# Expert results added through 0/1 lists in two fp32r passes, whole-tile places for weights, and the check for longer lists moved between two pairs

## The chip, the core and the metric

The kernel runs on one core of one Trainium2 chip. The metric is the device time of one execution in microseconds (us); smaller is better. Three runs of the kernel before gave a median of 688.06 us (687.87 to 689.03).

## What is computed

The reference is one layer of an encoder on 256 tokens of width 1024: a token mixer (two attention-like branches, merged and normalised), then a mixture of 16 experts. Only the second half is touched here:

```
logits = x @ router_w + router_b; probs = softmax(logits)
g_sel  = group of 4 experts that holds the largest prob
top 2 experts inside that group; their two gates are renormalised to sum 1
expert e on its rows xr:  h = silu(xr @ w1[e]) * (xr @ w3[e]);  y = h @ w2[e]
y_moe[token] = sum over its two experts of gate * y
x = layer_norm(ALPHA * x + y_moe)
```

All arrays are float32. Each expert has three 1024 x 1024 matrices, 12.6 MB, so that the sixteen experts are 201 MB of weights that are read once.

## The kernel before

**Front.** The first 240 us compute the mixer. There the matmuls run on fp32r operands: a number is split into a high part (rounded to fp32r) and a low remainder, and three matmuls (high by high, high by low, low by high: lines 186 to 188 and 199 to 201) replace one fp32 matmul.

**Experts.** The experts are done in eight pairs (loop over `e` = 0, 2, ..., 14, from about line 1454). Each expert has room for S = 64 tokens. `find(e)` (line 1252, VectorE) writes for the pair a tile `oneh` of 128 tokens x 256: for each of two token tiles and each of the pair's two experts, a 1 where the token's place in the expert's list equals the column. `gather` (line 1260) multiplies the tokens by these 0/1 columns, so that the pair's 128 rows lie as columns in `xg`. `gate_lists` (line 1275, VectorE) then multiplies the 0/1 lists by the gates, and `turn_lists` (lines 1280 and 1281) transposes them into `GT`. `up(e, m)` (line 1288) multiplies the rows of one expert by w1 (m = 0) or w3 (m = 2): 16 matmuls of 64 rows x 512 columns, whose two halves lie in the two column halves of the array. ScalarE and VectorE make the gated product `sg`, `turn_pe` (line 1296) transposes it, and ScalarE copies it to `hT`. `down(e, half)` (line 1305) multiplies by w2 into two PSUM banks `py`. These are copied to `y[0]` by ScalarE (line 1492) and `y[1]` by VectorE (line 1493), and in the next pair, after its first `up`, `combine` (line 1313) adds GT times y to the four accumulators `acc`: four fp32 matmuls of 128 x 512.

In the trace every fp32 matmul is two instructions (32 for one `up`, 8 for `combine`); an fp32r matmul is one.

**Weights.** A pair needs twelve tiles of 128 x 4096 (2 MB each): four for each expert's `up`, then four for `down`. There are eleven places for such tiles: three in `ring`, and one each in EA, E0, E1, E2, E3, GA, P1 and X. Five of them (E0, E1, E3, P1, X) are pools of four tiles of 128 x 1024. `load_exp(place)` (lines 846 to 875) takes the next tile of a fixed order into a place that has just been read for the last time: one transfer of 2 MB (rows of 16 KB; line 874), or, in a place of four tiles, four transfers of 512 KB (rows of 4 KB; `load_parts`, line 901). All are issued on the queue of SyncE (SP), in this order. The tile before the last four comes in four transfers (line 872), and the last four (w2 of experts 14 and 15) come in 24 smaller ones in turns (line 863), the last sixteen of 256 KB.

**Tail.** The last pair's `down2(c, fs)` (line 1324) makes the result in three column blocks, c = 0, 1, 2; `combine2(c)` (line 1331) adds each, and the final normalisation follows block by block (lines 1500 to 1550).

**Longer lists.** An expert can have more than 64 tokens. `gates` computes a flag `cfl` for that early. After `down2(0)` (line 1495) four engines load the flag into a register, and `tc.If` (line 1498) jumps over `more_slots()`, which handles the longer lists, when there are none. With the reference's data there are none. Seven places are named as its work space. A hint for the jump stands some instructions ahead of it (`mark_branch_hint_location`, line 1478).

The two lines of the loader that matter most:

```
elif pl in parts4:
    load_parts(e, m, pl, 4)
```

Of the kernel before, what the change touches and what calls it, by code (L numbers as in the profile page):

```python
# [25 lines left out]
LAST = NE - 2  # L26
# [19 lines left out]

@with_exitstack
def trunk(ctx: ExitStack, tc: tile.TileContext, x, cst_d, rows_d, wf, we, lvl_d, out):
# [16 lines left out]
    E0 = ctx.enter_context(tc.tile_pool(name="e0", bufs=4))  # L65
# [782 lines left out]
    def load_exp(pl, n=1):  # L848
        for _ in range(n):
# [15 lines left out]
            elif pl in parts4:  # L865
                load_parts(e, m, pl, 4)
            else:
                t = pl.tile([128, 4096], F32, name="w", tag="w")
                exl[e, m] = [t[:, i * 1024:(i + 1) * 1024] for i in range(4)]
                if nxt[0] == len(order) - 5:  # L870
                    for i in range(4):
                        nc.sync.dma_start(exl[e, m][i], we[e, m, :, i * 1024:(i + 1) * 1024])
                else:
                    nc.sync.dma_start(t, we[e, m])
# [6 lines left out]

    def slot(pl):

        if pl in parts4:
            return [part(pl) for _ in range(4)]
        t = pl.tile([128, 4096], F32, name="w", tag="w")
        return [t[:, i * 1024:(i + 1) * 1024] for i in range(4)]

    def part(pl):
        return pl.tile([128, 1024], F32, name="w", tag="p4" if pl is P1 else "w", bufs=4)  # L890
# [86 lines left out]
    def phase3():  # L977
# [3 lines left out]
        late["E1"] = ctx.enter_context(tc.tile_pool(name="e1", bufs=4))  # L981
# [27 lines left out]
    def phase4():  # L1009
# [3 lines left out]
        late["E3"] = ctx.enter_context(tc.tile_pool(name="e3", bufs=4))  # L1013
        load_exp(late["E2"])
        fr[14] = [late["E3"].tile([128, 1024], F32, name="w", tag="w") for _ in range(4)]
# [156 lines left out]
    hiT = [HI.tile([128, 512], F32, name=f"e{i}", tag="hi") for i in range(4)]  # L1172
    xg = [t.rearrange("p (k s) -> p k s", s=128) for t in hiT[0:2]]
    oneh = hiT[2][:, 0:256].rearrange("p (t a s) -> p t a s", t=2, a=2)
    oneh2 = hiT[2][:, 0:256].rearrange("p (t s) -> p t s", t=2)
    GT = hiT[2][:, 256:512].rearrange("p (t s) -> p t s", t=2)
    sg, hT, y = hiT[3], loT[0:2], loT[2:4]
    acc = [[bank("s" if tt else "o", [128, 512], f"acc{tt}{nh}") for nh in range(2)] for tt in range(2)]

    def residual(tt):  # L1180

        for nh in range(2):
            t = y[nh].rearrange("p (k s) -> p k s", s=128)
# [8 lines left out]
    def residual_add(tt):  # L1192
        for nh in range(2):
            t = y[nh].rearrange("p (k s) -> p k s", s=128)
# [104 lines left out]
    def down(e, half, py):  # L1299
        for f in range(4 * half, 4 * half + 4):  # L1300
            c0 = (f % 4) * 128 + (f // 4) * 64
            for nh in range(2):
                for a in range(2):
                    wt = exl[e + a, 4 + f // 4][f % 4]
                    PE.matmul(py[nh][64 * a:64 * a + 64, :], hT[a][:, c0:c0 + 64], wt[:, nh * 512:nh * 512 + 512],  # L1305
                              start=f == 0, stop=f == 7)
        for a in range(2):
            load_exp(home[e + a, 4 + half])

    def combine(start):  # L1310
        for tt in range(2):
            for nh in range(2):
                PE.matmul(acc[tt][nh], GT[:, tt, :], y[nh], start=start, stop=False, skip_group_check=True)  # L1313


    def down2(c, fs):
# [8 lines left out]
        if fs[-1] == 7:  # L1325
            A.copy(y[1][:, c * 256 - 256:c * 256] if c else y[0], W["y"])  # L1326

    def combine2(c):
        cs = slice(c * 256 - 256, c * 256) if c else slice(0, 512)
        for tt in range(2):  # L1330
            PE.matmul(acc[tt][c > 0][:, cs], GT[:, tt, :], y[c > 0][:, cs], start=False, stop=True,  # L1331
# [4 lines left out]
    def norm_params():  # L1336
# [3 lines left out]
        homes = [ring] * 3 + [EA, late["E2"], late["GA"]]  # L1340
        homes += parts4
        for p in (pl, home[LAST, 5], home[LAST + 1, 5]):
            homes.remove(p)
        par["w"] = homes
# [11 lines left out]
    def more_slots():  # L1356
# [4 lines left out]
        sh = sm[:, 64:66]  # L1361
        for e in range(NE):
            for m in range(6):
                for i in range(4):
                    G.dma_start(wt[m][i], we[e, m, :, i * 1024:(i + 1) * 1024])
            for b in range(2):
# [18 lines left out]
                V.tensor_copy(t2[:, 2:4, :], pg)  # L1385
                for fh in range(2):
                    h = {}
                    for m in (0, 2):
                        h[m] = bank("g", [128, 512])
                        for k in range(8):  # L1390
                            c = fh * 512
                            PE.matmul(h[m], t1[:, k, :], wt[m + k // 4][k % 4][:, c:c + 512], start=k == 0, stop=k == 7)
                    A.activation(sgm, h[0], AF.Sigmoid)
                    V.tensor_mul(hh, h[0], sgm)
                    V.tensor_mul(hh, hh, h[2])
# [3 lines left out]
                    V.tensor_copy(t3[:, 4 * fh:4 * fh + 4, :], pt)  # L1399
                for nh in range(2):  # L1400
                    py = bank("g", [128, 512])

                    n = 2 if e >= LAST and nh else 1
                    for q in range(n):
                        for f in range(8):
                            w = wt[4 + f // 4][f % 4][:, nh * 512:nh * 512 + 512]
                            if e >= LAST:
                                w = wt[5][2 * q + f // 4][:, f % 4 * 256:] if nh else wt[4][f // 2][:, f % 2 * 512:]
                            PE.matmul(py[:, q * 256:(q + 1) * 512 // n], t3[:, f, :], w[:, 0:512 // n],
                                      start=f == 0, stop=f == 7)  # L1410
                    V.tensor_copy(yb, py)
# [215 lines left out]
```

## Time and profile before

| what | value |
|---|---|
| median of 3 runs | 688.06 us (687.87 to 689.03) |
| profiled execution, its own time | 689.79 us |
| its span, first to last instruction | 688.0 us |
| mean granted TensorE clock | 0.991 of 2.4 GHz |
| TensorE matmul busy | 657.4 us (96%) |
| VectorE, ScalarE, GpSimd busy | 205.6, 187.7, 75.9 us |
| bytes moved by DMA | 238.71 MB, mean 347 GB/s |

A busy TensorE is not a TensorE at its peak: matmuls are pipelined and their ends are modelled. "Idle before, releaser" names what ended the idle time ahead of an instruction. The DMA share is the busy share of the core's sixteen DMA engines. SPq rows are issues of transfers, not the transfers themselves.

### The profile page before, as it was taken

The numbers are of one execution on the slowest core, as the hardware profiler recorded it, in microseconds if no ns is written. First come the engines' busy times: TensorE is split into PE (matmuls) and PEld (weight loads), VectorE is DVE, ScalarE is ACT, GpSimd is POOL, SyncE is SP. The second block draws the span as 40 slices with busy tenths as digits, with TensorE's granted clock in tenths as the row PEclk, the third lists the DMA queues.
The fourth block names the chain that finished last, engine by engine and source line by source line (L and its number), as shares of the span: only waits on it lengthen the run. The fifth ranks groups of instructions, "written<-read, shape, count | busy, mean of one in ns | idle before, by whom it ended". The sixth has DMA issues, their size and how long they took to land. (4 is left out here: it accounts for less than half of the span.)

```text
span 688.0 us, 9379 instructions
## 1 busy us (share of the span) xinstructions
PE 657.4 (96%) x3715; PEld 380.5 (55%) x3715; DVE 205.6 (30%) x469; ACT 187.7 (27%) x389; POOL 75.9 (11%) x74
## 2 busy tenths in 40 slices
PE   7999999999999999999999999999999998899976
PEld 6897988999989634344434433433533532334323
DVE  6788846454585311001001001001000100100015
ACT  5764466777464210120121100100100100011111
POOL 1113364431271000000000000000000000000001
PEclk9999999999999999999999999999999999999989
DMA  8969335538879699999999999999999999999971
GB/s 327 399 259 354 127 116 181 197 123 316 317 271 403 214 370 419 397 421 422 413 419 419 419 413 421 427 407 426 422 409 423 426 409 424 419 417 416 404 248 62
DMA packets 40517, 238.71 MB, mean 347 GB/s; under 512 B 4496, under 2 KB 4624, under 8 KB 32400
## 3 DMA queue, kind: packets, MB, share of 16 engines
q1 hardware_dynamic: 40464, 238.02, 86.5%
q8 instruction: 32, 0.52, 0.3%
q14 instruction: 21, 0.17, 0.1%
HBM read 236.95 MB, written 1.05 MB: 346 GB/s over the span
## 5 line engine op out<-in xcount | busy, mean ns | idle before, releaser
L1288 PE MATMUL g<-w,e 128*64 128x512 f32 x992 | 222.3, 598 | 3.5 <-DMA w<-in_we_dram 3.5
L1288 PEld LDWEIGHTS g<-w,e 128*64 128x64 f32 x992 | 69.7, 137 | 140.7 <-issue 126.9
L1305 PE MATMUL g<-w,f 128*64 128x512 f32 x448 | 105.7, 595 | 0.0
L166 DVE TENSOR_TENSOR lo<-w,hi 128x512 fp32r<-128x512 f32 x87 | 67.7, 789 | 51.0 <-ACT hi L165 50.1
L165 ACT CAST hi<-w 128x512 fp32r<-128x512 f32 x117 | 70.2, 618 | 39.2 <-PE g L200 31.8
L199 PE MATMUL g<-xp,hi 128*128 128x256 f32 x256 | 74.3, 290 | 0.0
L201 PE MATMUL g<-xp,lo 128*128 128x256 f32 x256 | 72.5, 283 | 0.2 <-DVE lo L166 0.2
L200 PE MATMUL g<-xp,hi 128*128 128x256 f32 x256 | 72.4, 283 | 0.0
L1305 PEld LDWEIGHTS g<-w,f 128*64 128x64 f32 x448 | 38.9, 137 | 56.5 <-issue 50.2
L166 POOL TENSOR_TENSOR lo<-w,hi 128x512 fp32r<-128x512 f32 x33 | 45.2, 1371 | 110.7 <-ACT hi L165 110.7
L1537 POOL TENSOR_TENSOR e<-e,par 128x256 f32<-128x256 f32 x2 | 1.4, 727 | 462.3 <-DVE nmr L1533 462.3
L199 PEld LDWEIGHTS g<-xp,hi 128*128 128x128 f32 x256 | 48.9, 191 | 2.6 <-issue 1.4
L201 PEld LDWEIGHTS g<-xp,lo 128*128 128x128 f32 x256 | 49.0, 191 | 0.4 <-DVE lo L166 0.4
L200 PEld LDWEIGHTS g<-xp,hi 128*128 128x128 f32 x256 | 49.0, 191 | 0.0
L1493 DVE COPY f<-g 128x512 f32<-128x512 f32 x7 | 4.8, 691 | 112.0 <-PE g L1305 112.0
L1260 PEld LDWEIGHTS g<-e,raw 128*128 128x128 f32 x224 | 26.1, 191 | 20.0 <-DVE e L1252 10.2
L1260 PE MATMUL g<-e,raw 128*128 128x128 f32 x224 | 28.7, 281 | 8.1 <-DVE e L1252 8.1
L1271 ACT ACTIVATE e<-g,cst 128x128 f32<-128x128 f32 x28 | 10.5, 456 | 64.5 <-PE g L1260 64.5
L1475 DVE TENSOR_TENSOR e<-e,g 128x512 f32<-128x512 f32 x8 | 5.5, 687 | 73.5 <-ACT e L1474 73.5
L1485 ACT COPY f<-g 128x512 f32<-128x512 f32 x8 | 4.7, 585 | 82.6 <-PE g L1296 82.6
L1313 PE MATMUL acc<-f,e 128*128 128x512 f32 x56 | 25.9, 605 | 0.0
L1462 DVE TENSOR_TENSOR e<-e,g 128x512 f32<-128x512 f32 x8 | 5.5, 688 | 64.1 <-PE g L1288 64.1
(316 smaller groups left out, 736.2 us busy)
## 6 DMA issues: line engine op xcount, KB each, us to landing
w<-in_we_dram SPq DMA_DIRECT2D x49, 2048.0 KB, 17.5
w<-in_we_dram SPq DMA_DIRECT2D x178, 512.0 KB, 11.0
w<-in_wf_dram SPq DMA_DIRECT2D x13, 2048.0 KB, 8.7
w<-in_wf_dram SPq DMA_DIRECT2D x8, 512.0 KB, 10.1
w<-in_we_dram SPq DMA_DIRECT2D x16, 256.0 KB, 5.6
rbc<-in_rows_dram SPq DMA_DIRECT2D x1, 1036.0 KB, 15.6
f<-in_we_dram SPq DMA_DIRECT2D x4, 256.0 KB, 7.1
out_dram<-par SPq DMA_DIRECT2D x4, 256.0 KB, 2.1
```

The costliest lines, as they stand in the source:

```text
L165: A.copy(hi, src)
L166: (G if on_pool(u) else V).tensor_sub(lo, src, hi.bitcast(F32))
L199: PE.matmul(p, hi[:, w], rh(k), start=k == 0, stop=False)
L200: PE.matmul(p, hi[:, w], rl(k), start=False, stop=False)
L201: PE.matmul(p, lo[:, w], rh(k), start=False, stop=k == nk - 1)
L1260: PE.matmul(p[:, i, :], raw[:, tt, k * 128:(k + 1) * 128], oneh2[:, tt, :], start=tt == 0, stop=tt == 1)
L1271: A.activation(t[:, i, :], p[:, i, :], AF.Identity, bias=C("b1")[:, 4 + i:5 + i], scale=C("g1")[:, 4 + i:5 + i])
L1288: PE.matmul(h[64 * nh:64 * nh + 64, :], xg[kh][:, k, 64 * (e % 2):64 * (e % 2) + 64], wcol(e, m + kh, k, nh), start=kh + k == 0, stop=kh = ...
L1305: PE.matmul(py[nh][64 * a:64 * a + 64, :], hT[a][:, c0:c0 + 64], wt[:, nh * 512:nh * 512 + 512], start=f == 0, stop=f == 7)
L1313: PE.matmul(acc[tt][nh], GT[:, tt, :], y[nh], start=start, stop=False, skip_group_check=True)
L1462: V.tensor_mul(sg, sg, h)
L1475: V.tensor_mul(sg, sg, h)
```

## The change

- E0, E1 and E3 become a `Place` each: one tile of 128 x 4096 with four parts. From the eighteenth tile of the order on (`WHOLE`), they are loaded by one transfer of 2 MB; P1 and X stay in four parts. By the order of the loader 21 tiles change from four transfers to one.
- The lists stay 0/1 and are held as fp32r (exactly). The gates are no longer multiplied into them (`gate_lists` is gone). Instead `turn_lists` multiplies the lists by the gate columns on TensorE (two matmuls with 2 columns), and ScalarE copies the gates of the 128 rows into `gs` (two copies of 64 x 1).
- `put_y(nh)` takes a half of the result out of PSUM, times `gs`, as a high part (ScalarE) and a low part (VectorE), both fp32r. `combine(nh)` adds it with four fp32r matmuls. The first half is added between the two halves of the next pair's `up(e, 0)`, the second after them.
- `find(e + 2)` moves ahead of `up(e + 1, 2)`.
- The check for longer lists moves from the tail to between pair 10 and pair 12 (`CHECK` = 12), behind both `combine`s, without the hint. Its work space is the two places of the w2 tiles (10, 5) and (11, 5), one in `ring` and P1; they are loaded again only after it. `more_slots` is rewritten to do with two places.

```
+class Place:
+    def __init__(self, ctx, tc, name):
+        self.t = ctx.enter_context(tc.tile_pool(name=name, bufs=1)).tile([128, 4096], F32, name="w")
+        self.at = 0
+    def part(self):
+        i, self.at = self.at, (self.at + 1) % 4
+        return self.t[:, i * 1024:(i + 1) * 1024]
...
-            elif pl in parts4:
+            elif pl in parts4 and (pl in (P1, X) or nxt[0] < WHOLE):
                 load_parts(e, m, pl, 4)
+            elif pl in parts4 and nxt[0] != len(order) - 5:
+                exl[e, m] = pl.parts()
+                nc.sync.dma_start(pl.t, we[e, m])
...
-    def gate_lists(e):
-        V.tensor_tensor(oneh, oneh, gw[:, :, e:e + 2][:, :, :, None].to_broadcast([128, 2, 2, S]), op=OP.mult)
-
-    def turn_lists():
-        p = bank("g", [128, 2, 128])
+    def turn_lists(e):
+        p = bank("g", [128, 260])
         for tt in range(2):
-            PE.transpose(p[:, tt, :], oneh2[:, tt, :], ident)
-        A.copy(GT, p)
+            PE.transpose(p[:, tt * 128:(tt + 1) * 128], oneh2[:, tt, :], ident)
+        for tt in range(2):
+            PE.matmul(p[:, 256:258], oneh2[:, tt, :], gw[:, tt, e:e + 2], start=tt == 0, stop=tt == 1)
+        A.copy(GT, p[:, 0:256].rearrange("p (t s) -> p t s", t=2))
+        for a in range(2):
+            r = slice(64 * a, 64 * a + 64)
+            A.copy(gs[r], p[r, 256 + a:257 + a])
...
+        if (e, half) == (CHECK - 2, 1):
+            return
         for a in range(2):
             load_exp(home[e + a, 4 + half])
-    def combine(start):
+    def put_y(nh):
+        if nh == 0:
+            y["h"], y["l"] = two("y", F32R)
+        A.activation(y["h"], py[nh], AF.Identity, scale=gs)
+        V.scalar_tensor_tensor(y["l"], py[nh], gs, y["h"].bitcast(F32), op0=OP.mult, op1=OP.subtract)
+
+    def combine(nh, start):
         for tt in range(2):
-            for nh in range(2):
-                PE.matmul(acc[tt][nh], GT[:, tt, :], y[nh], start=start, stop=False, skip_group_check=True)
+            for i in "hl":
+                PE.matmul(acc[tt][nh], GT[:, tt, :], y[i], start=start and i == "h", stop=False, skip_group_check=True)
...
+    def check_slots():
+        over = nc.values_load(cfl, engines=(ET.PE, ET.Activation, ET.DVE, ET.Pool), min_val=0, max_val=1)
+        pls = [home[CHECK - 2 + a, 5] for a in range(2)]
+        sl = [slot(pl) for pl in pls]
+        with tc.If(over > 0):
+            more_slots(*sl)
+        for pl in pls:
+            load_exp(pl)
...
     for e in range(0, NE, 2):
-        h = up(e, 0) if e else h0
+        if e == CHECK:
+            combine(0, False)
+            put_y(1)
+            combine(1, False)
+            check_slots()
+            h = up(e, 0)
+        elif e:
+            h = up(e, 0, (0,))
+            combine(0, e == 2)
+            put_y(1)
+            up(e, 0, (1,), h)
+        else:
+            h = h0
         A.activation(sg, h, AF.Sigmoid)
         V.tensor_mul(sg, sg, h)
-        if e:
-            combine(e == 2)
-        gate_lists(e)
+        if e not in (0, CHECK):
+            combine(1, e == 2)
...
+        if e < LAST:
+            find(e + 2)
         h = up(e + 1, 2)
-        if e == LAST:
-            tc.mark_branch_hint_location("slots", "LikelyTaken", engines=ENG4)
         V.tensor_mul(sg, sg, h)
         if e < LAST:
-            find(e + 2)
             p = gather(0)
...
-            A.copy(y[0], py[0])
-            V.tensor_copy(y[1], py[1])
+            put_y(0)
+    y[0], y[1] = two("y")
     down2(0, range(8))
-    over = nc.values_load(cfl, engines=(ET.PE, ET.Activation, ET.DVE, ET.Pool), min_val=0, max_val=1)
-    wt = [slot(pl) for pl in par["w"][0:7]]
-    tm = wt.pop()
-    with tc.If(over > 0, label="slots"):
-        more_slots()
     A.activation(sm[:, 90:91], eps_in[:, 0:1], AF.Sqrt)
```

## Rows read from the trace of the kernel before

**Rows 1.** The page, its parts 1 and 2: busy time, DMA share in 40 slices.

```profile
PE 657.4 (96%) x3715; PEld 380.5 (55%) x3715; DVE 205.6 (30%) x469; ACT 187.7 (27%) x389; POOL 75.9 (11%) x74
...
DMA  8969335538879699999999999999999999999971
```

**Rows 2.** Windows: stretch, length, busy by engine, PEclk, DMA share, GB/s.

```profile
250.00:653.00 403.00, 390.60 (x1852) 159.68 (x1850) 39.83 (x65) 43.35 (x93) 0.00 (x0) 1.00 1.01 417
...
560.00:575.00 15.00, 15.00 (x62) 5.16 (x61) 1.71 (x3) 0.97 (x2) 0.00 (x0) 1.00 1.02 408
575.00:590.00 15.00, 11.55 (x50) 3.67 (x50) 0.69 (x1) 1.18 (x2) 0.00 (x0) 0.90 1.02 428
653.00:668.00 15.00, 10.86 (x42) 4.13 (x39) 0.00 (x0) 2.07 (x3) 0.00 (x0) 0.81 0.86 300
```

**Rows 3.** Timeline of SP, 540 to 575 us: start, length, issues of weight transfers.

```profile
540.76 30.33 SPq L901 DMA_DIRECT2D w<-in_we_dram  x16
572.04 2.89 SPq L874 DMA_DIRECT2D w<-in_we_dram  x3
```

**Rows 4.** Timeline, 480 to 600 us: TensorE's pair 10 and its waits.

```profile
500.25 7.04 PE L1288 MATMUL g<-w,e 128*64 128x512 f32 x32
...
534.05 2.05 PE L1260 MATMUL g<-e,raw 128*128 128x128 f32 x16 [1.13 <-DVE e L1252]
...
553.18 7.04 PE L1288 MATMUL g<-w,e 128*64 128x512 f32 x32
...
585.88 5.35 PE L1288 MATMUL g<-w,e 128*64 128x512 f32 x16 [3.45 <-DMA w<-in_we_dram]
```

**Rows 5.** Timeline of TensorE's weight loads around one combine, 506 to 511 us.

```profile
506.26 0.14 PEld L1288 LDWEIGHTS g<-w,e 128*64 128x64 f32 x2 [0.28 <-issue]
507.22 0.30 PEld L1313 LDWEIGHTS acc<-f,e 128*128 128x128 f32 x2 [0.81 <-issue]
...
510.85 0.20 PEld L1288 LDWEIGHTS g<-w,e 128*64 128x64 f32 x4 [0.76 <-DMA w<-in_we_dram]
```

**Rows 6.** Timeline of TensorE in the front: fp32r matmuls, 512 columns.

```profile
105.09 0.39 PE L188 MATMUL g<-hi,xp 128*128 128x512 f32 x1
105.31 0.39 PE L186 MATMUL g<-hi,xp 128*128 128x512 f32 x1
```

**Rows 7.** Groups by line and shape: busy us, mean ns, idle before.

```profile
L1066 PE MATMUL g<-wg,rT 128*128 128x16 f32 x32 | 3.7, 258 | 0.0
...
L1456 ACT ACTIVATE e<-g 128x512 f32<-128x512 f32 x8 | 4.8, 597 | 49.6 <-PE g L1288 49.6
...
L1548 DVE SCALAR_TENSOR_TENSOR par<-par,sm,g 128x512 f32<-128x512 f32 x2 | 1.5, 732 | 0.0
```

**Rows 8.** Timeline of the tail, 657 to 677 us.

```profile
657.63 1.93 PE L1324 MATMUL g<-w,f 128*64 128x512 f32 x6 [0.21 <-DMA w<-in_we_dram]
...
663.34 3.68 PE L1324 MATMUL g<-w,f 128*64 128x256 f32 x16 [3.79 <-PEq L1498]
...
666.95 2.97 PE L1331 MATMUL acc<-f,e 128*128 128x512 f32 x4
...
669.86 2.81 PE L1324 MATMUL g<-w,f 128*64 128x256 f32 x24
...
672.60 1.13 PE L1331 MATMUL acc<-f,e 128*128 128x256 f32 x4
...
676.94 1.13 PE L1331 MATMUL acc<-f,e 128*128 128x256 f32 x4 [0.47 <-ACT f L1326]
```

**Rows 9.** Line 1498, the jump over the longer lists: ns min/median/max, first and last start.

```profile
L1498 DVEq COMPARE_BRANCH  x1: 81/81/81, 649.3 to 649.3; - x1
...
L1498 PEldq COMPARE_BRANCH  x1: 4651/4651/4651, 658.4 to 658.4; - x1
L1498 ACTq COMPARE_BRANCH  x1: 61/61/61, 660.0 to 660.0; - x1
```

**Rows 10.** Window behind TensorE's wait in the tail: columns as in rows 2.

```profile
663.00:668.00 5.00, 4.66 (x18) 2.48 (x19) 0.00 (x0) 0.00 (x0) 0.00 (x0) 0.50 0.74 271
```

More of the change, by code (lines that the diff above doesn't have):

```diff
@@ L44, with parts @@
 NR_COLS = _n
+class Place:
[5 more added lines that the diff above has]
+        return self.t[:, i * 1024:(i + 1) * 1024]
+    def parts(self):
+        self.at = 0
+        return [self.part() for _ in range(4)]
 @with_exitstack
@@ L880, in trunk @@
     SPLIT = 11
+    WHOLE = 18
+    whole = [None]
     def slot(pl):
@@ L885, in slot @@
             return [part(pl) for _ in range(4)]
-        t = pl.tile([128, 4096], F32, name="w", tag="w")
+        whole[0] = t = pl.tile([128, 4096], F32, name="w", tag="w")
         return [t[:, i * 1024:(i + 1) * 1024] for i in range(4)]
     def part(pl):
+        if isinstance(pl, Place):
+            return pl.part()
         return pl.tile([128, 1024], F32, name="w", tag="p4" if pl is P1 else "w", bufs=4)
@@ L1012, in phase4 @@
         late["E2"] = ctx.enter_context(tc.tile_pool(name="e2", bufs=1))
-        late["E3"] = ctx.enter_context(tc.tile_pool(name="e3", bufs=4))
+        late["E3"] = Place(ctx, tc, "e3")
         load_exp(late["E2"])
-        fr[14] = [late["E3"].tile([128, 1024], F32, name="w", tag="w") for _ in range(4)]
+        fr[14] = late["E3"].parts()
         for c in range(4):
@@ L1325, in down2 @@
         if fs[-1] == 7:
-            A.copy(y[1][:, c * 256 - 256:c * 256] if c else y[0], W["y"])
+            A.activation(y[1][:, c * 256 - 256:c * 256] if c else y[0], W["y"], AF.Identity, scale=gs)
     def combine2(c):
@@ L1330, in combine2 @@
         for tt in range(2):
-            PE.matmul(acc[tt][c > 0][:, cs], GT[:, tt, :], y[c > 0][:, cs], start=False, stop=True,
+            PE.matmul(acc[tt][c > 0][:, cs], GT[:, tt, :].bitcast(F32), y[c > 0][:, cs], start=False, stop=True,
                       skip_group_check=True)
@@ L1361, in more_slots, with load @@
         sh = sm[:, 64:66]
+        def load(e, m):
+            for i in range(4):
+                G.dma_start(wt[i], we[e, m, :, i * 1024:(i + 1) * 1024])
         for e in range(NE):
-            for m in range(6):
-                for i in range(4):
-                    G.dma_start(wt[m][i], we[e, m, :, i * 1024:(i + 1) * 1024])
             for b in range(2):
@@ L1385, in more_slots @@
                 V.tensor_copy(t2[:, 2:4, :], pg)
-                for fh in range(2):
[L1387 to L1395, printed above, removed]
+                h = [[bank("g", [128, 512]) for fh in range(2)] for i in range(2)]
+                for m in range(4):
+                    load(e, m)
+                    for fh in range(2):
+                        for k in range(4):
+                            PE.matmul(h[m // 2][fh], t1[:, m % 2 * 4 + k, :], wt[k][:, fh * 512:fh * 512 + 512],
+                                      start=m % 2 + k == 0, stop=m % 2 == 1 and k == 3)
+                for fh in range(2):
+                    A.activation(sgm, h[0][fh], AF.Sigmoid)
+                    V.tensor_mul(hh, h[0][fh], sgm)
+                    V.tensor_mul(hh, hh, h[1][fh])
                     pt = bank("g", [128, 4, 128])
@@ L1399, in more_slots @@
                     V.tensor_copy(t3[:, 4 * fh:4 * fh + 4, :], pt)
-                for nh in range(2):
[L1401 to L1411, printed above, removed]
+                o = [bank("g", [128, 512]) for nh in range(2)]
+                for m in range(2):
+                    load(e, 4 + m)
+                    if e < LAST:
+                        for nh in range(2):
+                            for f in range(4):
+                                PE.matmul(o[nh], t3[:, 4 * m + f, :], wt[f][:, nh * 512:nh * 512 + 512],
+                                          start=m + f == 0, stop=m == 1 and f == 3)
+                    else:
+                        for q in range(m + 1):
+                            n = 256 if m else 512
+                            for f in range(8):
+                                w = wt[2 * q + f // 4][:, f % 4 * 256:] if m else wt[f // 2][:, f % 2 * 512:]
+                                PE.matmul(o[m][:, q * n:q * n + n], t3[:, f, :], w[:, 0:n], start=f == 0, stop=f == 7)
+                for nh in range(2):
+                    V.tensor_copy(yb, o[nh])
                     for tt in range(2):
                         PE.matmul(acc[tt][nh], t2[:, 2 + tt, :], yb, start=False, stop=True, skip_group_check=True)
+    def check_slots():
[6 more added lines that the diff above has]
+            load_exp(pl)
     find(0)
```

44 lines of the change are left out of this document (23 added, 21 removed).

## The prediction

> **What bounds the kernel now.** I read the page first, then windows, then the timelines of SP, of TensorE and of its weight loads, and the tail last. On the page TensorE is busy for 96% of the span, and the sixteen DMA engines show 9s from slice 15 almost to the end [rows 1]. So two resources look full, and the question is which of them sets the end. From 250 to 653 us the DMA share is 1.01 at 417 GB/s [rows 2]: the weight stream never pauses. TensorE takes 52.93 us for pair 10 (553.18 - 500.25) [rows 4], but the stream needs 12 x 2.097 MB / 417 GB/s = 60 us for a pair's twelve tiles. TensorE lives on the tiles that were loaded before it began; when these are used up it waits, first for 3.45 us at 582 us [rows 4]. So the stream sets the time of the last pair, and TensorE follows it closely. SP confirms it: it issues the four four-part tiles from 540.76 to 571.1 us, long after their places had been read, at the pace of the stream [rows 3].
>
> Behind the stream comes a chain on TensorE. `down2(0)` ends at 659.56 (657.63 + 1.93), TensorE stands still for 3.79 us at the jump of line 1498, and the three blocks follow until the last `combine2` at 676.94 [rows 8]; normalisation takes the rest, and the change leaves it alone.
>
> **Whole tiles: the stream.** The 16 transfers of 512 KB issued up to 571.1 [rows 3] moved in 560 to 575 us at 408 GB/s; behind them come transfers of 2 MB, and 575 to 590 us show 428 GB/s at the same share of 1.02 [rows 2]. A tile of 2.097 MB thus takes 5.14 us in four parts and 4.90 us whole. 21 tiles change: 21 x 0.24 = **5.0 us** earlier. Bounds: 0, if the rate has another reason than the size of the transfers, and 6 us. I take 5.0, because both rates lie side by side in one stage. A whole transfer waits for the last quarter of its place and lands at once, so its first quarter comes up to 3 x 1.2 us later to TensorE; the last five tiles keep their small transfers, so this costs nothing at the end. As to the rule: the Trainium skill (DMA: Bandwidth & Descriptors, Specifications) gives 512 bytes as the least transfer for full rate. By that, rows of 4 KB and 16 KB would be equally fast and this term zero. The trace speaks against it, with 408 and 428 GB/s.
>
> **The tail without the check.** Removed: the 3.79 us stand. Behind it the granted clock is 0.50, the lower level of 1.2 GHz [rows 10], so that 16 matmuls of `down2` and the change to `combine2` take 3.61 us (663.34 to 666.95), where 24 at 2.4 GHz take 2.74 us (669.86 to 672.60) and 16 would take 1.8. That gives 1.8 us, and the first `combine2`, at mixed clock 2.91 us (666.95 to 669.86) instead of some 2.4 by rows 5, another 0.5 [rows 5, 8]. Sum **6.1 us**. Next in line are the last sixteen small transfers: 4.2 MB at 300 GB/s [rows 2] is 14 us, from 653 to 667. Half of them, which the first block needs, have moved by 660, when TensorE would now start it, and the last are needed at about 668, before the stream's 5.0 us are counted. Both have moved with it. Bounds of this term: 3.8 (no gain by the clock, or a wait for the last landings) to 6.5. The new scale in the copy of `y` is the same kind of instruction as before (0.6 us) [rows 7].
>
> **The check between the pairs.** Now TensorE stands there instead. It waits for `put_y(1)`, which must wait until `combine(0)` has read the tiles: 0.60 us on ScalarE and 0.73 on VectorE [rows 7], 1.4 us with the handovers. The jump costs 3.8 us as in the tail; its hint is gone, and I bound it by 0 and 6 us. The clock falls: after the 3.45 us wait 16 matmuls took 5.35 us [rows 4] where 32 take 7.04, that is 1.8 us more, and up to 2.7 after this longer stand. Sum 7.5 us (2 to 11). Queued behind the check on SP are the tiles for the two places it uses. In `ring` the check takes the free buffer, so the next load takes the one after it and waits for `up(12, 0)` to be read as well. SP comes to that load only at about 572 us [rows 3] (567 after), and TensorE would be through by about 562. So the stream does not stop. Four engines jump; GpSimd, ScalarE and VectorE have nothing due then.
>
> **TensorE's pairs.** Before, `combine` takes 3.63 us for eight instructions with one way back (507.22 to 510.85), plus 0.53 for the way in (0.96 instead of 0.43) [rows 5]: eight at 0.43 and 0.72 for the two switches between 64-column and 128-column use. fp32r matmuls of 512 columns follow each other in 0.22 to 0.23 us (105.09, 105.31) [rows 6], so eight take 1.8 instead of 3.4: -1.6. The second visit adds +0.7. The gate product adds four tiny instructions: 3.7 / 32 = 0.12 each [rows 7], +0.45. `find` earlier removes the wait ahead of `gather`, 1.13 us, and the drain beside it, about -1.3 [rows 4]. Together -1.8 us for pairs 2 to 10, -0.9 for pair 0, -2.5 for pair 12 (one visit), -0.5 for pair 14. The two small copies of the gates on ScalarE (under 0.6 us each) lie beside `up(e + 1, 0)`; `put_y(0)` lies under the first half of `up(e, 0)`, and `put_y(1)` under the second, 3.5 us each. By the tile at which TensorE waits now, -0.9 - 5 x 1.8 - 1.2 + 7.5 = -3.6 us: it comes there at 578.8 instead of 582.4. The tile lands at 585.9 - 18 x 0.24 = 581.6 (18 of the 21 come before). So TensorE still waits, and pairs and check together cost and bring **0** at the end. If this cover is gone, each us of the check beyond 2.8 more counts in full.
>
> **Sum.** -5.0 - 6.1 + 0 = -11.1 us. The profiled execution took 689.79 us (span 688.0 and 1.79 around it), so 678.7; the median of the runs lies 1.73 us lower, 688.06, and gives **677.0 us**.
>
> **Rivals.**
> - **The stream does not get faster**: the page's rule on 512 bytes holds, or the lower rate has to do with the places. Then only the tail counts: 688.06 - 6.1 = 682.0. Against it stand the two windows. 0.14.
> - **TensorE's stand in the tail is not the jump**, but the wait for small transfers that have moved and not yet been signalled. For it: the same jump took 81 ns on VectorE and 61 ns on ScalarE [rows 9]. Against it: on TensorE the jump itself is recorded with 4651 ns, from 658.4. Then the tail brings nothing: 688.06 - 5.0 = 683.1. 0.10. The Trainium skill (Advanced Engine Details and Errata, Control Flow Timing) has about 108 ns for a compare-and-branch; by that the jump would explain none of the 3.79 us, as in this rival. TensorE's row differs from it by a factor of 40.
> - **TensorE becomes the bound** from pair 12 on: fp32r adds no faster than fp32 here (the change then doesn't do what it says), or its tiles arrive so that it cannot use its lead. It would come 3 to 5 us late to the last pair: about 681. 0.10.
> - **Slower**: the jump without its hint, in the midst of the stream, keeps TensorE while its next instructions are fetched behind weights. It takes place once, at pair 12. Beyond 10.3 us for the whole check (7.5 + 2.8), each us counts; the gain of 11.1 is used up at 21.4, and slower by 0.2% is reached at 22.8. At 25 us it would be 691.7. Against it: the only such jump of the trace cost 4.65 us under the same stream. 0.05.
>
> **How the numbers follow.** The forecast, 677.0 with its own range of 674.5 to 679.5, has 0.58. The rest, 0.03, is for no change. The rivals between 681 and 683.1 lie on the same side, so the range goes from 674.0 to 683.0. One run to the next tells about 0.2%, 1.4 us. Faster: 0.58 + 0.14 + 0.10 + 0.10 = 0.92; same 0.03; slower 0.05.
>
> **What would show it.** The stream: windows without a stretch of four part-tiles near 408 GB/s, and the last weights landing about 5 us earlier. The tail: no wait for line 1498, a clock of 1.0 through `down2(1)`, and about 11.5 us from the end of `down2(0)` to the last `combine2` instead of 17.4. The check: one stand of TensorE near 550 us, followed by a lower clock, and thereafter waits for weights, not for places. Combine: eight instructions about 0.23 us apart. I would be wrong if the whole transfers showed no more than 410 GB/s, if TensorE showed no wait for weights behind pair 12, or if SP waited for the check's places while the DMA share fell.

## The result and the profile after

The changed kernel takes **679.27 us** (median of 4 runs, 678.38 to 680.05), the kernel before took 688.54 us beside it (4 runs, 687.87 to 689.41): ratio 0.9869, 95% interval 0.9844 to 0.9894, or 9.3 us less. The forecast was 677.0 us with a range of 674.0 to 683.0. The sign and the main mechanisms held; one term of the sum was too large, and the reasoning behind another failed. One of the six runs of x9 below went at a granted clock of 0.85 instead of 0.99 and took 732.72 us; it is left out of its numbers.

The profiled execution took 680.05 us (span 678.3), 9.74 us less than that of before. First the page, then windows (stretch, length, busy by engine, PEclk, DMA share, GB/s):

```profile
PE 651.0 (96%) x3747; PEld 389.8 (57%) x3747; DVE 208.5 (31%) x468; ACT 195.3 (29%) x412; POOL 75.9 (11%) x74
...
DMA  8969325636879599999999999999999999999992
```

```profile
250.00:653.00 403.00, 390.43 (x1904) 168.44 (x1904) 43.84 (x66) 50.89 (x117) 0.00 (x0) 0.99 1.01 421
653.00:668.00 15.00, 14.44 (x87) 8.40 (x84) 4.03 (x10) 3.12 (x5) 0.00 (x0) 1.00 0.65 232
663.00:668.00 5.00, 4.44 (x31) 2.96 (x31) 1.42 (x4) 0.47 (x1) 0.00 (x0) 1.00 0.04 15
```

The DMA share is 1.01 as before, but the same share now moves 421 instead of 417 GB/s [rows 2]. In the tail TensorE is busy for 14.44 of 15 us at the full clock, where it was busy for 10.86 at 0.81. From 663 us on next to nothing is moved any more, where the DMA share was still 0.74 [rows 10]: the last weights land earlier, as forecast.

Next TensorE in pair 10, at the check and behind it (start, length, what it does, idle before and what ended it):

```profile
496.54 1.21 PE L1355 MATMUL acc<-y,e 128*128 128x512 f32 x4
497.68 3.65 PE L1321 MATMUL g<-w,e 128*64 128x512 f32 x16
501.27 1.21 PE L1355 MATMUL acc<-y,e 128*128 128x512 f32 x4
...
520.15 8.78 PE L1321 MATMUL g<-w,e 128*64 128x512 f32 x32 [2.13 <-DMA w<-in_we_dram]
...
534.83 7.05 PE L1338 MATMUL g<-w,f 128*64 128x512 f32 x30 [2.48 <-DMA w<-in_we_dram]
...
550.90 0.51 PE L1355 MATMUL acc<-y,e 128*128 128x512 f32 x1
551.68 0.97 PE L1355 MATMUL acc<-y,e 128*128 128x512 f32 x3 [0.28 <-DVE y L1350]
553.20 0.50 PE L1355 MATMUL acc<-y,e 128*128 128x512 f32 x1 [0.54 <-ACT y L1349]
553.99 0.98 PE L1355 MATMUL acc<-y,e 128*128 128x512 f32 x3 [0.28 <-DVE y L1350]
560.92 15.87 PE L1321 MATMUL g<-w,e 128*64 128x512 f32 x64 [5.96 <-PEq L1467]
...
581.60 10.52 PE L1321 MATMUL g<-w,e 128*64 128x512 f32 x48
...
602.23 2.05 PE L1290 MATMUL g<-e,raw 128*128 128x128 f32 x16
```

A visit to `combine` is now four instructions in 1.21 us, twice per pair. The first waits for weights come in pair 10 (2.13 and 2.48 us); before, the first came in pair 12, at 582 us [rows 4]. Then the check: the two visits with their handovers, and a stand of 5.96 us charged to line 1467, the jump. Behind it TensorE has no wait for weights until the tail; the prediction had named this as a sign of being wrong. The stand in windows:

```profile
555.00:560.00 5.00, 0.00 (x0) 0.00 (x0) 0.00 (x0) 0.00 (x0) 0.00 (x0) 0.80 0.99 412
560.00:565.00 5.00, 4.08 (x10) 1.38 (x12) 0.00 (x0) 0.00 (x0) 0.00 (x0) 0.52 1.00 402
```

TensorE does nothing for five microseconds, and the granted clock behind that is 0.52, almost all of the stretch at the lower level of 1.2 GHz. The DMA share stays at 0.99 to 1.00: the stream does not stop for the check, as forecast.

The tail (same columns as TensorE's timeline above):

```profile
657.49 1.98 PE L1373 MATMUL acc<-y,e 128*128 128x512 f32 x4
659.40 3.45 PE L1366 MATMUL g<-w,f 128*64 128x256 f32 x24
662.78 1.13 PE L1373 MATMUL acc<-y,e 128*128 128x256 f32 x4
663.84 2.92 PE L1366 MATMUL g<-w,f 128*64 128x256 f32 x24
667.32 1.13 PE L1373 MATMUL acc<-y,e 128*128 128x256 f32 x4 [0.56 <-ACT y L1368]
```

The wait of 3.79 us and the slow `combine2` of 2.97 us [rows 8] are gone. `down2(0)` ends at about 655.9 (657.49 less the 16 matmuls of the next block, 1.6), the last `combine2` starts 11.4 us later; before it was 676.94 - 659.56 = 17.4. So of the 9.7 us between the two profiled executions, 6.0 lie in the tail and 3.6 ahead of it (659.56 to 655.9).

### The profile page after: what moved, and what is told of

It reads as the page before. It is cut to its first block, busy times and chain, and to the rows that moved or that the text cites. A ratio compares the mean times of both kernels' runs of the same rounds, so it can differ in the third digit from the quotient of the medians.

```text
span 678.3 us, 9336 instructions
## 1 busy us (share of the span) xinstructions
PE 651.0 (96%) x3747; PEld 389.8 (57%) x3747; DVE 208.5 (31%) x468; ACT 195.3 (29%) x412; POOL 75.9 (11%) x74
## 5 line engine op out<-in xcount | busy, mean ns | idle before, releaser
L1338 PEld LDWEIGHTS g<-w,f 128*64 128x64 f32 x448 | 40.9, 137 | 56.0 <-issue 51.8
L1350 DVE SCALAR_TENSOR_TENSOR y<-g,sm,y 128x512 fp32r<-128x512 f32 x14 | 10.5, 750 | 140.5 <-ACT y L1349 140.5
L1290 PEld LDWEIGHTS g<-e,raw 128*128 128x128 f32 x224 | 26.1, 191 | 11.4 <-issue 11.4
L1544 DVE TENSOR_TENSOR e<-e,g 128x512 f32<-128x512 f32 x8 | 5.5, 687 | 76.3 <-ACT e L1543 76.3
L1349 ACT ACTIVATE y<-g,sm 128x512 fp32r<-128x512 f32 x14 | 9.6, 687 | 61.3 <-PE g L1338 28.4
L203 PE MATMUL g<-lo,xp 128*128 128x512 f32 x48 | 19.7, 411 | 1.5 <-DVE lo L182 1.1
```

What stands on the lines that cost most here:

```text
L203: PE.matmul(p, rh(c)[:, t], lo[:, a:b], start=False, stop=False, skip_group_check=True)
L1290: PE.matmul(p[:, i, :], raw[:, tt, k * 128:(k + 1) * 128], oneh2[:, tt, :], start=tt == 0, stop=tt == 1)
L1350: V.scalar_tensor_tensor(y["l"], py[nh], gs, y["h"].bitcast(F32), op0=OP.mult, op1=OP.subtract)
```

## Experiments

Each kernel below ran beside the kernel before on the same chip. They are grouped by the question. The kernel before had medians of 687.7 to 688.1 us there and 688.54 beside the changed kernel, so a difference of two medians taken at different times is uncertain by nearly 1 us; ratios to the kernel before are the safer measure.

### Is it the whole tiles that make the stream faster?

**x1_parts**: the changed kernel with all four-part places loaded in four parts.

```
-    WHOLE = 18
+    WHOLE = 1000
```

> The changed kernel, but E0, E1 and E3 keep four transfers of 512 KB for every tile (the kernel after took 679.3 us, the one before 688.5). Theory: 21 whole tiles made the weight stream faster (408 against 428 GB/s), and that is the part of the gain that is not the tail's. Then TensorE waits for weights again behind pair 12, the last weights land about 4 us later, and the time is 682 to 683 us. Rival: the stream gained because TensorE frees its places earlier; then the form of the transfers is nothing and the time stays at 679.3.

Measured: 682.51 us (681.58 to 685.21, 6 runs), ratio 0.9931 [0.9909, 0.9953], 3.2 us above the changed kernel (4.3 by the two ratios) and with no overlap of the intervals. The window and two rows of TensorE:

```profile
250.00:640.00 390.00, 376.22 (x1828) 160.33 (x1824) 41.79 (x63) 49.22 (x112) 0.00 (x0) 0.98 1.01 417
```

```profile
534.23 9.75 PE L1338 MATMUL g<-w,f 128*64 128x512 f32 x30 [3.86 <-DMA w<-in_we_dram]
...
563.24 15.79 PE L1321 MATMUL g<-w,e 128*64 128x512 f32 x64 [6.17 <-PEq L1467]
```

The rate is back at 417 GB/s (the changed kernel has 422 in the same window), TensorE waits longer for weights in pair 10 (3.86 instead of 2.48 us), and the `up` behind the check begins 2.3 us later (563.24 against 560.92). So the transfers are the cause, and not the new places as such. The waits behind pair 12 that were expected did not come: behind the check TensorE stands for no weights here either, and what it lost in pair 10 stays to the end.

**x10_halves**: two transfers of 128 partitions with rows of 8 KB.

```
-                nc.sync.dma_start(pl.t, we[e, m])
+                for i in range(2):
+                    nc.sync.dma_start(pl.t[:, i * 2048:i * 2048 + 2048], we[e, m, :, i * 2048:i * 2048 + 2048])
```

> The changed kernel with the 21 tiles of E0, E1 and E3 loaded by two transfers of 128 partitions and rows of 8 KB, instead of one with rows of 16 KB or four with rows of 4 KB (which gave 679.3 and 682.5 us). Theory (the rate goes with the length of a row, by a fixed cost per row): with 408 GB/s at 4 KB and 428 at 16 KB a row costs 10.04 ns per KB at 4 KB rows of one core's stream against 9.57, so a fixed part is spread over twice the bytes: at 8 KB the tile takes about 4.98 us instead of 5.14 or 4.90, 421 GB/s in their stretches, 250 to 640 us at 420 to 421 GB/s and about 680.2 us (679.5 to 681). Rival (only the transfer that fills a whole place is fast): like four parts, 682.5 us and 417 GB/s. Second rival (8 KB is already long enough): 679.3 us and 422 GB/s.

Measured: 679.57 us (678.89 to 680.89, 6 runs), ratio 0.9889 [0.9865, 0.9914], 420 GB/s from 250 to 640 us. The rival with 682.5 us is out. The other two lie 0.9 us apart, and by the time they can't be told; the rate, between 417 and 422, leans to a fixed cost (the 10.04 and 9.57 ns of its theory are per 4 KB, not per KB). Whether that cost is one per row or one per transfer is not shown: four, two and one transfers of 128 rows each give the same three values either way. Two transfers of 1 MB have most of the gain by the median (2.9 of 3.2 us) and some three fifths of it by the rate.

**x5_rows**: four transfers of 32 partitions each, with whole rows of 16 KB.

```
-                nc.sync.dma_start(pl.t, we[e, m])
+                for i in range(4):
+                    nc.sync.dma_start(pl.t[32 * i:32 * i + 32, :], we[e, m, 32 * i:32 * i + 32, :])
```

> The changed kernel, but the 21 whole tiles come in four transfers of 512 KB that hold 32 partitions each, with rows of 16 KB (in the kernel before a quarter held all 128 partitions, with rows of 4 KB). Theory: the length of the rows sets the rate; then windows inside the expert stage show 425 GB/s or so as after, and the time is that of the changed kernel, 679.3 us. Rival: the size or the number of the transfers sets it; then they show 405 to 410 GB/s in the stretches of four-part tiles and the time is that with four parts, 682.5 us.

Measured: 852.98 us (842.93 to 876.31, 6 runs), ratio 1.2324 [1.2275, 1.2373]; no theory had this. Two windows of it, the first while other tiles are loaded, the second while these are:

```profile
500.00:510.00 10.00, 10.00 (x46) 3.46 (x44) 1.38 (x2) 1.38 (x2) 0.00 (x0) 1.00 1.01 427
520.00:530.00 10.00, 3.73 (x19) 1.57 (x16) 0.69 (x1) 0.57 (x3) 0.00 (x0) 0.71 0.98 207
```

At the same share of "busy" the engines move half as much. So a long row is not enough: a transfer over 32 partitions loses far more than the row gains. Numbers of partitions between 32 and 128 were not run, and why 32 run at half the rate was not settled.

### What does the check cost, and where?

**x2_nocheck**: the changed kernel without the jump and the block; the order around it and the late reload of its two places stay. **x3_before_nocheck**: the kernel before without the check in the tail and its hint.

```
-        over = nc.values_load(cfl, engines=(ET.PE, ET.Activation, ET.DVE, ET.Pool), min_val=0, max_val=1)
         pls = [home[CHECK - 2 + a, 5] for a in range(2)]
-        sl = [slot(pl) for pl in pls]
-        with tc.If(over > 0):
-            more_slots(*sl)
```

```
-    over = nc.values_load(cfl, engines=(ET.PE, ET.Activation, ET.DVE, ET.Pool), min_val=0, max_val=1)
-    wt = [slot(pl) for pl in par["w"][0:7]]
-    tm = wt.pop()
-    with tc.If(over > 0, label="slots"):
-        more_slots()
```

> The changed kernel without the check for longer lists (the jump and the work behind it are left out; the two places are loaded again at the same point). Theory: with the check TensorE stands 10 us at pair 12 and is itself the bound from there on, some 1.4 us behind the weights. Without it TensorE waits for weights to the end, and the time is 677.5 to 678.2 us. Rival: the missing 1.4 us of the forecast were lost at the start of the experts, where the stream began 2 us later; then the check costs nothing and the time stays at 679.3.

> The kernel before, without the check for longer lists in its tail (left out altogether). Theory: TensorE's stand of 3.8 us and the half clock behind it go, 6.0 us, to 682.5 us. Rival: TensorE stands there because its small transfers have not landed; then the time stays at 688.5.

Measured: x2 677.90 us (677.44 to 678.5, 4 runs), ratio 0.9854 [0.983, 0.9878]; x3 683.61 us (681.85 to 684.56, 6 runs), ratio 0.9932 [0.9911, 0.9953]. Three differences follow. The check in the tail cost 688.07 - 683.61 = **4.5 us** (688.07 is the median of before beside these two). Whole tiles and the new adding, compared without any jump, bring 683.61 - 677.90 = **5.7 us**. The jump between the pairs costs 679.27 - 677.90 = **1.4 us** (the waits for `put_y` are in both); the two ranges of single runs overlap by 0.1 us, and by the ratios, whose intervals overlap, it is 1.0 us. In x3 TensorE goes from `down2(0)` into the next block without a stand:

```profile
652.96 9.80 PE L1324 MATMUL g<-w,f 128*64 128x512 f32 x48
```

Without the check TensorE does wait for weights in pair 12, as in these rows of x2:

```profile
550.07 0.50 PE L1355 MATMUL acc<-y,e 128*128 128x512 f32 x1
...
577.96 3.65 PE L1321 MATMUL g<-w,e 128*64 128x512 f32 x16 [1.33 <-DMA w<-in_we_dram]
582.76 3.65 PE L1321 MATMUL g<-w,e 128*64 128x512 f32 x16 [1.15 <-DMA w<-in_we_dram]
...
592.70 8.75 PE L1338 MATMUL g<-w,f 128*64 128x512 f32 x30 [2.87 <-DMA w<-in_we_dram]
601.38 2.05 PE L1290 MATMUL g<-e,raw 128*128 128x128 f32 x16
```

These waits pay for the jump. From the first visit at the check to the `gather` behind the first `down` of pair 12 it takes 51.3 us without the jump (550.07 to 601.38) and 51.3 us with it (550.90 to 602.23 in the changed kernel). So in these two executions the check costs nothing up to there, but nothing is to spare either; the 1.4 us are a difference of medians, and where they arise was not traced.

**x4_check8**: the check two pairs earlier.

```
-    CHECK = 12
+    CHECK = 8
```

> The changed kernel with the check between pairs 6 and 8 instead of 10 and 12. Theory: TensorE pays the same 10 us, but at a time when it is not yet waiting for weights; the waits that come later (4.6 us in pair 10, and those at the end) shrink by as much, and the time is that without a check, 677.5 to 678.2 us. Rival (the check costs nothing where it is): 679.3. Third: so early it lets the places stand empty, and the time is longer, above 680.

Measured: 678.33 us (677.89 to 678.72, 4 runs), ratio 0.9863 [0.984, 0.9887]. The jump is recorded with 6.43 us there, but TensorE meets the stream again in pair 12 and waits:

```profile
452.04 16.45 PE L1321 MATMUL g<-w,e 128*64 128x512 f32 x64 [6.49 <-PEq L1467]
...
592.25 7.05 PE L1338 MATMUL g<-w,f 128*64 128x512 f32 x30 [2.82 <-DMA w<-in_we_dram]
```

The waits in pair 10 are gone in its trace and those of pair 12 remain, so the stand was paid out of waits that would have come anyway. Of the versions that compute everything, this one has the lowest median, 0.9 us below the changed kernel; the intervals of the two overlap.

**x9_tail**: the changed kernel with the check put back behind `down2(0)`, its hint with it.

```
-        if e == CHECK:
-            combine(0, False)
-            put_y(1)
-            combine(1, False)
-            check_slots()
-            h = up(e, 0)
-        elif e:
+        if e:
...
     down2(0, range(8))
+    check_slots()
```

> The changed kernel with the check put back behind down2(0), its hint some instructions ahead, two free places as work space; the pairs run without it and the tiles (10, 5) and (11, 5) reload their places at once. Theory: TensorE's stand and the low clock behind it come back in the tail, +6.0 us there, and the 1.4 us that the check costs between the pairs are saved: 679.3 + 6.0 - 1.4 = 683.9 us (682.5 to 685). Stand of 3.5 to 6.5 us charged to the check's line; from the end of down2(0) to the last combine2 about 17 us. Rival (the stand in the tail was a wait for the small transfers, not the jump; the whole tiles land earlier, so it is gone): 678 to 679.5 us, about 11.5 us from down2(0) to the last combine2.

Measured: 682.46 us (681.95 to 685.31, 5 runs), ratio 0.9935 [0.9908, 0.9962]: 4.6 us above x2 (5.6 by the ratios), where 6.0 were expected. In its tail (TensorE's timeline, then the rows of the jump's line: ns min/median/max, first and last start):

```profile
657.62 2.79 PE L1364 MATMUL g<-w,f 128*64 128x256 f32 x16 [2.87 <-DMA w<-in_we_dram]
660.34 2.78 PE L1371 MATMUL acc<-y,e 128*128 128x512 f32 x4
...
670.24 1.13 PE L1371 MATMUL acc<-y,e 128*128 128x256 f32 x4 [0.57 <-ACT y L1366]
```

```profile
L1465 PEldq COMPARE_BRANCH  x1: 4191/4191/4191, 653.0 to 653.0; - x1
```

From the end of `down2(0)` (646.93 + 7.83) to the last `combine2` it takes 15.5 us, where 17 were expected; in x2 it takes 10.7. The stand is back, and 4.6 us of time with it: with x3, the jump is the cause, and the rival of a mere wait for transfers is out. The releaser of this wait is given as a DMA, but the jump's record of 4.19 us spans it, from 653.0 to 657.2, and the last sixteen matmuls begin 0.4 us behind.

### What makes the jump long?

**x6_hint**: the hint for the jump is given again, in the up of expert 11 (`mark_branch_hint_location` when `e == CHECK - 2`). **x7_check8_hint**: the same with `CHECK = 8`.

```
-        with tc.If(over > 0):
+        with tc.If(over > 0, label="slots"):
...
+        if e == CHECK - 2:
+            tc.mark_branch_hint_location("slots", "LikelyTaken", engines=ENG4)
```

> The changed kernel with the jump's hint given again, ahead of the second up of expert 11. The jump took 4.65 us on TensorE before (with hint, in the tail) and 5.82 us after (without). Theory: the hint is worth that difference, TensorE stands 1.2 us less at pair 12, where it is the bound, and the time is about 678.2 us. Rival: the hint is worth nothing, since the same jump with it cost nearly as much; 679.3 us and 5.8 us on TensorE.

> The check between pairs 6 and 8, and the hint for its jump. Theory: with the check at pair 8 its price is covered by later waits for weights, so a shorter jump brings nothing more: 678.3 us as with the check at 8 alone. Rival: every stand of TensorE costs also there; then about 1.2 us less, 677.1.

Measured: x6 679.55 us (677.76 to 681.83, 6 runs), ratio 0.9885 [0.9861, 0.9909]; x7 678.51 us (678.4 to 679.26, 4 runs), ratio 0.9862 [0.9839, 0.9885]. With the hint TensorE's jump is recorded with 6.26 us (at pair 12) and 6.15 us (at pair 8), without it with 5.82 and 6.43. The hint does nothing measurable here. The execution of x6 also sets a price on the check at pair 12, for it begins the experts as early as that of x2, which has no check; the first row is of x2, the others of x6:

```profile
236.33 3.65 PE L1487 MATMUL g<-w,e 128*64 128x512 f32 x16
...
236.41 3.65 PE L1491 MATMUL g<-w,e 128*64 128x512 f32 x16
...
560.39 15.65 PE L1321 MATMUL g<-w,e 128*64 128x512 f32 x64 [6.32 <-PEq L1467]
```

Their spans are 676.7 and 676.8 us: a stand of 6.32 us cost 0.1 us in this execution. The six runs of x6 spread over 4 us, though, and their median lies 1.65 us above that of x2.

The rows of the jump's line in the changed kernel led further:

```profile
L1467 POOLq EVENT_SEMAPHORE  x4: 17/43/43, 252.9 to 253.1; - x4
L1467 POOLq COMPARE_BRANCH  x1: 51/51/51, 247.4 to 247.4; - x1
...
L1467 DVEq COMPARE_BRANCH  x1: 81/81/81, 553.6 to 553.6; - x1
L1467 PEldq COMPARE_BRANCH  x1: 5821/5821/5821, 554.8 to 554.8; - x1
L1467 DVEq EVENT_SEMAPHORE  x1: 21/21/21, 559.1 to 559.1; - x1
L1467 PEldq EVENT_SEMAPHORE  x1: 51/51/51, 560.7 to 560.7; - x1
```

The jump is recorded with 51 and 81 ns on GpSimd and VectorE, but the next event of each comes 5.5 us after it, about as late as on TensorE (5.9). The front has a jump of the same kind (line 620), which TensorE records with 0.40 us. One thing in which the two differ is what they jump over.

**x11_block32**: the skipped block cut to one of its 32 turns. **x12_block0**: cut to four instructions, one for each engine.

```
-        for e in range(NE):
-            for b in range(2):
+        for e in range(1):
+            for b in range(1):
```

```
-            more_slots(*sl)
+            wt, tm = sl
+            p = bank("g", [128, 128])
+            V.tensor_copy(tm[0][:, 0:128], ident)
+            PE.transpose(p, tm[0][:, 0:128], ident)
+            A.copy(tm[1][:, 0:128], p)
+            G.tensor_copy(wt[0][:, 0:128], tm[1][:, 0:128])
```

> The changed kernel with the skipped block cut to one of its 32 turns (a list of up to 128 rows of expert 0 alone would be handled, which is the part left out; with these data the block is never entered). Everything ahead of the jump and behind it stays. Theory (the stand is the way to the instructions behind a long skipped block: on three engines the next recorded event comes 5.4 to 5.9 us after the jump, while the front's jump of line 620 is recorded with 0.40 us): with a block 32 times shorter the stand falls below 2 us, and with the lower clock behind it the check costs nothing any more: 678 us, as without the check (677.4 to 678.6). Rival (the jump has its price whatever it skips): stand of 5.5 to 6.5 us and 679.3 us (678.7 to 680).

> The changed kernel with the skipped block cut to four instructions, one for each engine (longer lists are not handled at all, which is the part left out; the block is never entered). Theory (length of the skipped block): stand under 1 us, near the 0.40 us of the front's jump, and 677.4 to 678.5 us. Second theory (it is a matter of the nearest instructions: a block of 1/32 is still too long, one of four instructions is not): the stand stays in the run with 1/32 and is gone here. Rival (the jump has its price whatever it skips): stand of 5.5 to 6.5 us and 679.3 us.

Measured: x11 677.56 us (676.78 to 678.57, 6 runs), ratio 0.9847 [0.9815, 0.9879]; x12 677.54 us (676.37 to 679.34, 6 runs), ratio 0.985 [0.9817, 0.9883]. Of x11, the matmuls behind the jump, and then rows of the jump's line:

```profile
554.46 13.95 PE L1321 MATMUL g<-w,e 128*64 128x512 f32 x64 [0.47 <-PEq L1467]
...
592.10 7.05 PE L1338 MATMUL g<-w,f 128*64 128x512 f32 x30 [2.83 <-DMA w<-in_we_dram]
```

```profile
L1467 DVEq COMPARE_BRANCH  x1: 81/81/81, 552.6 to 552.6; - x1
L1467 DVEq EVENT_SEMAPHORE  x1: 21/21/21, 553.0 to 553.0; - x1
L1467 PEldq COMPARE_BRANCH  x1: 423/423/423, 553.7 to 553.7; - x1
```

The stand fell from 5.96 to 0.47 us, VectorE's gap from 5.5 to 0.4 us, and the 64 matmuls behind take 13.95 instead of 15.87 us because the clock stays up (1.00 from 555 to 565 us). The time is that of the kernel without the check. In x12 the record is 0.24 us and TensorE shows no stand. So **the length of the block that is skipped makes the jump long**, not the jump itself. What an engine does on its way past a long block, no run here shows.

### Does the adding in fp32r matter?

**x8_fp32**: the results are added by one fp32 matmul each, without the low part.

```
-            for i in "hl":
-                PE.matmul(acc[tt][nh], GT[:, tt, :], y[i], start=start and i == "h", stop=False, skip_group_check=True)
+            PE.matmul(acc[tt][nh], GT[:, tt, :].bitcast(F32), y["h"], start=start, stop=False, skip_group_check=True)
```

> The changed kernel with the results added in fp32 (one matmul of two instructions instead of two fp32r matmuls; the low part on VectorE is left out), at the same two places per pair. It costs TensorE 1.6 us more per pair. Theory: up to pair 10 the waits for weights (6.3 us with the clock) cover most of five times 1.6; from pair 12 on TensorE is the bound and the last two pairs' 3.2 us count: 682 to 684 us. Rival: TensorE's time in the pairs does not matter because the weights set the end: 679.3 us. Third: it matters everywhere: 7 x 1.6 more, 690 us.

Measured: 680.82 us (680.21 to 681.5, 4 runs), ratio 0.9899 [0.9876, 0.9923], 1.5 us above the changed kernel. One visit in pair 10, and the start behind the check:

```profile
501.40 1.98 PE L1353 MATMUL acc<-y,e 128*128 128x512 f32 x4
...
560.38 15.37 PE L1321 MATMUL g<-w,e 128*64 128x512 f32 x64 [5.15 <-PEq L1465]
```

A visit takes 1.98 instead of 1.21 us, so a pair costs 1.54 us more, 7.7 over pairs 2 to 10. But the waits for weights in pair 10 are gone from the trace: 2.13 + 2.48 us, and the 1.7 us by which the 32 matmuls at 520.15 ran longer than 7.09. That is 6.3 of the 7.7 us, and 1.4 are left. That this lies close to the 1.5 measured is partly chance: behind the check the visits there and in pair 14 cost some 2.3 us more, while the stand is 0.8 us shorter and the matmuls behind it 0.5 us. The 682 to 684 us that were expected counted these later visits in full and missed. Time that TensorE saves ahead of pair 10 is mostly handed to the stream.

## Why the prediction held, and where it did not

- **What bounds the kernel** held: the stream, with TensorE close behind it, at the same DMA share of 1.01.
- **Whole tiles, -5.0 us**: 417 to 422 GB/s by the windows; 5.7 us measured together with the adding, without checks in the way (x3 against x2), and with the pairs put at 0. With the check between the pairs 3.2 us of it show by the medians and 4.3 by the ratios (x1); TensorE then has no wait for weights behind pair 10, so that it is late by itself. The Trainium skill (DMA: Bandwidth & Descriptors, Specifications) gives 512 bytes as the least transfer for full rate; by that x1 would have been as fast as the changed kernel, and the runs with 4, 8 and 16 KB (682.5, 679.6 and 679.3 us) speak against it. The rival of a stream that gets no faster is out; that it is the row, and not the number of transfers, is not shown.
- **The tail, -6.1 us**: 6.0 between the two profiled executions, with the clock at 1.00 behind it, as forecast. But by medians the check in the tail was worth 4.5 us (x3) and 4.6 us (x9 against x2). The term was priced from one execution, in which the jump took 4.65 us and fell so that 3.79 were left as a stand; in x9 2.87 were left. **It was mis-sized by some 1.5 us against the median**, though 6.1 still lies at the edge of what the interval of x3 allows (3.2 to 6.1 us). The rival that put the stand down to late signals is out (x3, x9).
- **The check between the pairs, "0 at the end"**: this is the step whose reasoning failed. Its price was put at 7.5 us (1.4 for `put_y(1)`, 3.8 for the jump, 1.8 to 2.7 for the clock). Measured: 560.92 - 550.90 less the two visits of some 2 us, or 8 us, and 1.9 for the clock (15.87 against 13.95 in x11), 10 in all; the stand at the jump is 5.96 us instead of 3.8, within the bounds of 0 to 6. That alone would still have been covered by the 2.8 us spare. What was wrong is the lead behind it: "TensorE still waits" was worked out by adding up -0.9, five times -1.8 and -1.2 ahead of 582.4 us, as though each us saved in a pair could be kept. In the trace TensorE ran into the stream in pair 10 already and stood there for 4.6 us, with the clock lower behind it. Its lead was gone before the check began. It came to the tile of the forecast at about 588.6 us (581.60 and two thirds of 10.52) instead of 578.8, 2.2 us of which are a later start, and from the check on it had no wait for weights until the tail. That the check cost little even so is not the forecast's cover but another: waits for weights that x2 still has in pair 12. In the traces they pay for all of it (51.3 us with and without the jump; x6 against x2), with nothing to spare; by medians 1.4 us are left, and x4, x11 and x12 get most or all of that back by an earlier place or a shorter block. So the 0 came out nearly right, by luck in part. TensorE without a wait behind pair 12 is the second half of the rival "TensorE becomes the bound", at a smaller price than the 3 to 5 us put on it.
- **TensorE's pairs**: -1.8 us each was about right. From the first `up` of pair 8 to that of pair 10 it is 493.01 - 442.21 = 50.8 us against 52.93 [rows 4], that is -2.1. A visit of four fp32r matmuls takes 1.21 us, which is 0.23 each [rows 6] and some 0.3 for the switch.
- **SP and the places** held: the share stays at 0.99 and more through the check.
- **The rival "slower"** rested on a jump without its hint. The hint changes nothing (x6, x7).

By medians the sum is: tail -4.5 instead of -6.1, tiles and pairs -5.7 instead of -5.0, check +1.4 instead of 0: -8.8 us against -11.1. These terms are differences along one chain of medians, so they must add up to the measured -9.3 but for the 0.5 us between two medians of before; the sum is no check of its own.

A place where profile and page differ is the jump. TensorE records 5821 ns for it over the long block and 235 ns over the block of four instructions. The Trainium skill (Advanced Engine Details and Errata, Control Flow Timing) has about 108 ns for a compare-and-branch: that is of the size of the records of 51 to 81 ns on the other three engines, and it says nothing of the gap behind them.

## What to carry to other kernels

A jump over a long block that is hardly ever entered is not free even when it is skipped (4 to 6 us of TensorE here): look at the time to the next event of every engine, not at the record of the branch, and shorten the block or put the jump where waits that come later would have taken the time anyway. When an engine runs just behind a stream, a saving ahead of their meeting point can't be carried past it: work out the lead anew from each wait for weights. Load large tiles with few transfers over all partitions (here 1 or 2 MB each, rows of 8 or 16 KB), and test a split of a transfer before trusting its row length.

## What the runs showed of the hardware beyond that

- A transfer of 32 partitions x 16 KB moves at about half the rate of one of 128 partitions x 16 KB (207 against 427 GB/s) at a DMA share of 0.98: the share tells that engines are taken, not that they move much.
- The skipped block's length sets the way past it: 5.8 us for 32 turns on TensorE, 0.42 for one, 0.24 for four instructions; ScalarE went on in 0.5 us (552.8 to 553.3) even over the long block, and why is open.
- The start of the experts moves from one execution to the next. At 222 to 238 us the router's narrow matmuls run, and the granted clock there differs: 1.00 from 228 to 234 us in the profiled execution of before, 0.72 in that of after (a part of the stretch at 1.2 GHz), 0.50 (all of it) in x3:

```profile
228.00:234.00 6.00, 5.90 (x34) 5.12 (x36) 1.39 (x5) 0.78 (x2) 0.00 (x0) 0.72 0.10 38
```

```profile
228.00:234.00 6.00, 6.00 (x31) 6.00 (x30) 1.15 (x5) 0.00 (x0) 0.00 (x0) 0.50 0.05 17
```

The first row is of the changed kernel, the second of x3. The first `up` behind it began at 235.1 us in the kernel before, 237.3 in the changed one and 239.0 in x3, and the stream is nearly idle meanwhile (DMA share 0.10 and 0.05), so that a late start can be carried to the end. It may be a part of the spread of 1 to 6 us between runs of one kernel, which is not shown, since one execution of each was traced; it does make a single execution a poor scale for a term of 1 us, unless two begin alike.
